# Two splits of the memory's weights, traced two steps later in the last pair's attention tail

## The chip, the cores and the metric

The kernel runs on one core of a Trainium2 chip. The metric is the device time of one execution in microseconds (us). TensorE is PE in the profile, its weight loads are PEld, VectorE is DVE, ScalarE is ACT, GpSimd is POOL, and SyncE, which issues the transfers here, is SP.

## The reference

One layer of a streaming encoder runs for two request groups with the same weights: a prompt of 1024 rows and a sample of 64 rows with caches. All inputs are float32. What matters for the change:

```
h = rms_norm(x, g_norm1)
qa, ka, va, qb, kb, vb, logf = in_proj(h, w_in, ...)       # 8 heads A, 8 heads B
oa = chunk_band_attn(qa, ka, va, rel_bias)                 # heads A
ob = forget_attn(qb, kb, vb, logf)                         # heads B: causal, logit += c[t] - c[s]
x = x + concat(oa, ob) @ w_o
kv = rms_norm(mem, g_mem) @ w_mkv                          # mem: 256 x 1024, w_mkv: 1024 x 2048
mk, mv = rms_norm(kv[:, :1024]), kv[:, 1024:]
x = x + mem_attend(rms_norm(x, g_norm2), mk, mv, w_mq, g_mq, w_mo)
x = x + conv_ffn(rms_norm(x, g_norm3), ..., w_up, w_conv, b_conv, w_down)
```

## The kernel before, in words

Every float32 product is made of three matmuls on two-part operands: an operand is split into a rounded high part and the rest, its low part (`hi` and `lo` in the names), and `SPLIT` lists the products hi·hi, hi·lo, lo·hi. A split takes a cast on ACT (the high part) and a subtraction on DVE or POOL (the low part).

The heads are worked in eight pairs. For a pair and a group of 256 query rows, attention has these steps, each a small function:

- `Attn.score` (lines 474 to 509): for heads B, POOL adds the forget term to a bias row (L485, `s<-bias,ctok`) and masks the diagonal block (L486). PE makes the scores (L499, `S<-kh,q`) in a PSUM tile `S` of which there is one. DVE adds bias and scores and takes the maximum (L502, `s,mx<-S,s`), ACT takes the exponential (L504), DVE the reciprocal of the sum (L505), and POOL (L507) or ACT (L509) divides by it.
- `Attn.turn` (L539 to L541): PE transposes the probabilities (`PT<-ident,s`), ACT and DVE split them into `pth` and `ptl`.
- `Attn.sum` (L554 to L566): PE multiplies them with the values into the PSUM tile `O`, of which there is one; ACT copies one half out (L563, `otmp<-O`), DVE adds the halves (L564, `mix<-O,otmp`), and a transfer stores `mix` to DRAM. The next head's L554 can write `O` only when L564 has read it.

The last pair's attention is left over when the projections are done. It is worked in four leftover steps, `LEFT = (0, 0, 0, 15)`: `step(n, substeps())` interleaves the steps of attention with `n` pieces of the next stage. In front of these steps the memory stage is opened: `load_mem` loads the memory's rows (a tile `s`) and splits them into `mhi` and `mlo` (L265, L266: `gained`), and `load_wm(n, z)` loads half a block of `w_mkv` into `mwraw` (two buffers, 512 KB each, L661). `split_wm(n, y)` splits a quarter of block `n`:

```
    def split_wm(n, y):
        raw = wraw[n, y // 2][:, 2 * (y % 2):2 * (y % 2) + 2]
        hi = mp.tile([P, 2, 256], F32R, name="mwhi", bufs=6)
        lo = mp.tile([P, 2, 256], F32R, name="mwlo", bufs=6)
        act.copy(hi, raw)
        (dve if y % 2 else pool).tensor_tensor(lo, raw, f32(hi), op=ALU.subtract)
```

The cast is L668 and the subtraction L669. The products of the memory stage (L679, `pj<-mwhi,mhi` and the like) are 16 units of 24 matmuls, cut into 64 pieces, of which 15 belong to the last leftover step and the rest to the sample attention that follows (`Sample`, L720 to L851: keys `kraw`, L740, split at L774 and L775). A unit's end (L695 to L713) makes a normed row `kv`, and PE transposes it at L710 during the next unit.

The order of the text is not the order on the engines. A scheduler in the framework places the traced instructions: it takes them by their place in the trace and by when it expects their inputs, and fixes a row of instructions for each engine and for SP. On the chip each engine runs its row in order and waits at a semaphore where an input is late. So a call that is traced elsewhere can move its neighbours too.

Of the kernel before, what the change touches and what calls it, by code (L numbers as in the profile page):

```python
# [26 lines left out]
LEFT = (0, 0, 0, 15)  # L27
# [14 lines left out]
def hybrid_step(ctx: ExitStack, tc: tile.TileContext, i: dict, o: dict):  # L42
# [3 lines left out]
    def f32(ap):  # L46
        return ap.bitcast(F32)
# [522 lines left out]
    def substeps(slow=False):  # L570

        sc = todo[0].scores() if todo else []
        va = late.pop(0).values() if late else []
        if todo:
            late.append(todo.pop(0))
        ns, ts = [x for x, _ in turns], [x for _, x in turns]
        turns.clear()
        first = held[:]
        held[:] = ts if slow else []
        r = first[:1] + ns + first[1:] + sc[:1] + ends if slow else first + sc[:1] + ends + ns  # L580
        r += va[:1] + sc[1:] + va[1:-1] + ([] if slow else ts)
        ends[:] = va[-1:]
        return [f for f in r if f]
# [69 lines left out]
    def load_mem(z):  # L653
        raw = wk.tile([P, N], F32, name="s", bufs=4)[:, :1024].rearrange("p (k t) -> p k t", k=4)
        nc.sync.dma_start(raw, i["memT"][4 * z:4 * z + 4].rearrange("k p t -> p k t"))
        for k in range(4):
            gained((mem[0][:, 4 * z + k], mem[1][:, 4 * z + k], raw[:, k], gcol[:, 3, 4 * z + k:4 * z + k + 1], ALL))
# [6 lines left out]
# [6 lines that stand above are left out]
        wm.setdefault(n, []).append((hi, lo))  # L670
# [201 lines left out]
    def step(n, subs):  # L872
        weave(line[:n], subs)
        del line[:n]
# [2 lines left out]
    load_mem(0)  # L877
    load_wm(0, 1)
    load_mem(1)
    split_wm(0, 0)  # L880
    split_wm(0, 1)
    for n in LEFT:
        step(n, substeps())
    assert not (todo or late or turns or ends)
    heads.close()
# [409 lines left out]
    def long_row(tag):  # L1295
        return row(tag, 768)[:, :H]
# [27 lines left out]
    for w, m in enumerate(ROWS):  # L1324
        x = long_row("qhi")
        nc.sync.dma_start(x, x1d[m, :, 0:H])
        for q in range(2):
            n = 2 * w + q
# [148 lines left out]
    for n, m in enumerate(ROWS):  # L1477
        x = long_row("qhi")
# [415 lines left out]
```

## Time and profile before

| | |
|---|---|
| time, median of 3 runs | 1781.4 us (1781.03 to 1784.44) |
| profiled execution | 1788.58 us, of which the span is 1786.6 us |
| mean granted TensorE clock | 0.988 |
| PE busy | 1717.5 us (96%) |
| DVE, ACT, POOL busy | 1210.5, 941.2, 647.3 us |
| last pair's attention tail, about 571 to 599 us | PE busy 0.38 of the first 8 us, 4.73 of the next 6, 10.82 of the last 14 |

The profiled execution is 7.2 us longer than the median of the runs; differences are worked out against the profiled execution and then taken off the median. In the timelines below the columns are: start in us, duration in us, engine, line, operation, output<-input, and in brackets the idle time of the engine before it and what ended it. With `x3` the row merges three instructions in a row, and the duration is that of all.

### The profile page before, as it was taken

The numbers are of one execution on the slowest core, as the hardware profiler recorded it, in microseconds if no ns is written. First come the engines' busy times: TensorE is split into PE (matmuls) and PEld (weight loads), VectorE is DVE, ScalarE is ACT, GpSimd is POOL, SyncE is SP. The second block draws the span as 40 slices with busy tenths as digits, with TensorE's granted clock in tenths as the row PEclk, the third lists the DMA queues.
The fourth block names the chain that finished last, engine by engine and source line by source line (L and its number), as shares of the span: only waits on it lengthen the run. The fifth ranks groups of instructions, "written<-read, shape, count | busy, mean of one in ns | idle before, by whom it ended". The sixth has DMA issues, their size and how long they took to land.

```text
span 1786.6 us, 33930 instructions
## 1 busy us (share of the span) xinstructions
PE 1717.5 (96%) x12432; PEld 1668.3 (93%) x12432; DVE 1210.5 (68%) x2643; ACT 941.2 (53%) x2058; POOL 647.3 (36%) x931
## 2 busy tenths in 40 slices
PE   7898999999998898999999999999999999999999
PEld 6888999999997777999999999999999999999999
DVE  5768667677677686433444369877777777649986
ACT  6756667677677577433555456434333333434432
POOL 4556667778777443453443612100000000000000
PEclk8999999999999999999999999999999999999999
DMA  7322222122112777541111563222222222693332
GB/s 251 91 62 64 60 77 78 49 74 76 51 56 83 216 252 219 165 143 56 54 54 60 151 214 104 79 75 77 79 85 85 85 73 73 216 346 130 118 104 88
DMA packets 134391, 199.87 MB, mean 112 GB/s; under 512 B 20984, under 2 KB 74360, under 8 KB 134224
## 3 DMA queue, kind: packets, MB, share of 16 engines
q1 hardware_dynamic: 134224, 197.70, 35.0%
q8 instruction: 98, 1.61, 0.4%
q14 instruction: 69, 0.57, 0.1%
HBM read 155.35 MB, written 45.44 MB: 112 GB/s over the span
## 4 chain that ended last, share of the span: by engine, by line
PE 46%; DVE 4%; issue 2%; ACT 1%; POOL 1%; DMA 1%; SPq 0%; DVEq 0%; ACTq 0%; POOLq 0%
PE W L1449 24%; PE W L1773 11%; PE pj L937 7%; PE S L1192 1%; PE tq L1228 1%; PE O L1228 1%; POOL lo L920 1%; DVE f L1314 0%; PE PT L1215 0%; DMA f<-x2d 0%; DVE lo L920 0%; DMA h<-ad 0%; PE O L1192 0%; ACT hi L1313 0%; DVE qhi L1301 0%
## 5 line engine op out<-in xcount | busy, mean ns | idle before, releaser
L299 PE MATMUL pj<-whi,xhi 128*128 128x384 f32 (+1 forms) x512 | 195.8, 382 | 2.7 <-DVE flog L314 1.6
L299 PE MATMUL pj<-wlo,xhi 128*128 128x384 f32 (+1 forms) x512 | 177.0, 346 | 4.3 <-POOL wlo L123 4.3
L299 PE MATMUL pj<-whi,xlo 128*128 128x384 f32 (+1 forms) x512 | 175.9, 344 | 0.7 <-DVE xlo L131 0.7
L1555 POOL COPY s<-gp 128x2 f32<-128x2 f32 x22 | 15.8, 720 | 335.8 <-DVE gp L1554 335.8
L1449 PE MATMUL W<-h,hi 128*128 128x272 f32 x704 | 134.4, 288 | 1.4 <-ACT qlo L1585 1.4
L504 ACT ACTIVATE s<-s,mx 128x640 f32<-128x640 f32 (+7 forms) x128 | 94.4, 737 | 77.4 <-DVE mx L502 76.5
L1773 PE MATMUL W<-f,hi 128*128 128x272 f32 x672 | 127.1, 287 | 0.1
L541 DVE TENSOR_TENSOR ptl<-PT,pth 128x512 fp32r<-128x512 f32 (+2 forms) x192 | 99.4, 522 | 37.5 <-ACT pth L540 35.3
L1449 PEld LDWEIGHTS W<-h,hi 128*128 128x128 f32 x704 | 110.8, 188 | 1.6 <-ACT qlo L1585 1.6
L540 ACT CAST pth<-PT 128x512 fp32r<-128x512 f32 (+2 forms) x192 | 84.7, 449 | 41.7 <-PE PT L539 39.9
L1773 PEld LDWEIGHTS W<-f,hi 128*128 128x128 f32 x672 | 105.3, 188 | 0.4 <-DVE f L1520 0.4
L299 PEld LDWEIGHTS pj<-wlo,xhi 128*128 128x128 f32 x512 | 99.5, 194 | 5.9 <-POOL wlo L123 5.9
L299 PEld LDWEIGHTS pj<-whi,xhi 128*128 128x128 f32 x512 | 99.4, 194 | 4.3 <-DVE flog L314 1.9
L1449 PE MATMUL W<-h,lo 128*128 128x272 f32 x352 | 101.8, 289 | 0.0
L299 PEld LDWEIGHTS pj<-whi,xlo 128*128 128x128 f32 x512 | 98.3, 192 | 1.4 <-DVE xlo L131 1.2
L1773 PE MATMUL W<-f,lo 128*128 128x272 f32 x336 | 96.7, 288 | 0.0
L539 PE MATMUL PT<-ident,s 128*128 128x128 f32 x528 | 89.9, 277 | 6.9 <-DVE ptl L541 5.4
L1313 ACT CAST hi<-raw 128x512 fp32r<-128x512 f32 x68 | 42.2, 621 | 98.6 <-PE W L1449 59.2
L499 PE MATMUL S<-kh,q 128*128 128x256 f32 (+1 forms) x304 | 77.8, 281 | 13.5 <-DVE mx L502 13.5
L937 PE MATMUL pj<-a,hi 128*128 128x384 f32 (+1 forms) x352 | 89.3, 337 | 0.2 <-DMA mraw<-mixd 0.2
L507 POOL TENSOR_SCALAR s<-s,ssum 128x640 f32<-128x640 f32 (+6 forms) x96 | 70.8, 738 | 47.9 <-DVE ssum L505 34.3
L554 PE MATMUL O<-pth,v 128*128 128x256 f32 (+1 forms) x304 | 76.5, 277 | 8.5 <-DVE mix L564 7.7
(538 smaller groups left out, 6037.6 us busy)
## 6 DMA issues: line engine op xcount, KB each, us to landing
raw<-in_w_down_dram SPq DMA_DIRECT2D x45, 256.0 KB, 2.8
wraw<-in_w_dram SPq DMA_DIRECT2D x56, 192.0 KB, 2.5
raw<-in_w_up_dram SPq DMA_DIRECT2D x41, 256.0 KB, 2.8
h<-ad SPq DMA_DIRECT2D x32, 272.0 KB, 5.5
mwraw<-in_w_mkv_dram SPq DMA_DIRECT2D x16, 512.0 KB, 6.1
raw<-in_w_mo_dram SPq DMA_DIRECT2D x32, 256.0 KB, 3.2
kvraw<-in_w_down_dram SPq DMA_DIRECT2D x32, 256.0 KB, 3.0
ad<-t SPq DMA_DIRECT2D x22, 272.0 KB, 2.2
```

The source lines that it names most:

```text
L299: pe.matmul(pj[:, :nw], x2[a][:, k, t * P:(t + 1) * P], wt[k][b][:, :nw], start=n == 0, stop=n == 3 * KT - 1)
L499: pe.matmul(sp[:, a:a + (k1 - k0) * P], q, kk[:, h, src], start=m == 0, stop=m == 1)
L504: act.activation(s[:, :n], s[:, :n], ACT.Exp, bias=mx, scale=-1.0, accum_out=sm)
L507: pool.tensor_scalar(s[:, :n], s[:, :n], sm, 1.0, op0=ALU.mult, op1=ALU.mult)
L539: pe.transpose(pt[:, b - ch[0]], self.s[j][:, (b - w0) * P:(b - w0 + 1) * P], ident)
L540: act.copy(hi[:, f:f + n, j], pt[:, f:f + n])
L541: dve.tensor_tensor(lo[:, f:f + n, j], pt[:, f:f + n], f32(hi[:, f:f + n, j]), op=ALU.subtract)
L554: pe.matmul(op[:, cols], groups[p, b // 2].v[:, b % 2, h].rearrange("p a d -> p (a d)"), pt[:, x, cols], start=b == self.full[0] and m == ...
L937: pe.matmul(out()[:, :cn], w[a][:, k % 4], x[b][k][:, c0:c0 + cn], start=k == 0 and n == 0, stop=k == KT - 1 and n == 2)
L1313: act.copy(hi, t)
L1449: pe.matmul(w[:, z, :Q], a(p, j), rights[j][b][:, z * Q:z * Q + Q], start=fresh and begin and j == 0 and x == 0, stop=final and end and j ...
L1773: pe.matmul(ws[m][:, z, :Q], la[p][:, m * P:(m + 1) * P], ra[b][:, z * Q:z * Q + Q], start=first and y == 0 and what in opening, stop=fina ...
```

## The change

The first two of the memory's splits, `split_wm(0, 0)` and `split_wm(0, 1)`, are traced in front of the third leftover step instead of in front of the first. The rest of the opening (the loads, and the splits of the memory's rows) stays where it was.

```diff
     load_mem(0)
     load_wm(0, 1)
     load_mem(1)
-    split_wm(0, 0)
-    split_wm(0, 1)
-    for n in LEFT:
+    for x, n in enumerate(LEFT):
+        if x == 2:
+            split_wm(0, 0)
+            split_wm(0, 1)
         step(n, substeps())
```

No instruction is added or taken away. The rows of all engines differ only from this place on, until early in the product with `w_o` about 150 us later. From line 880 on the changed kernel's line numbers are higher by one; line numbers here are those of before.

ACT, from the splits of the first half of the memory's rows (`mhi`) on, before:

```order
L265 ACTIVATE mhi<-s,gcol 128x256 x3
L668 CAST mwhi<-mwraw 128x512 x2
L563 COPY otmp<-O 64x256
L540 CAST pth<-PT 128x4x128 x2
L668 CAST mwhi<-mwraw 128x512 x2
L265 ACTIVATE mhi<-s,gcol 128x256 x4
L504 ACTIVATE s,ssum<-s,mx 128x896
```

ACT at the same place after:

```order
L265 ACTIVATE mhi<-s,gcol 128x256 x3
L563 COPY otmp<-O 64x256
L540 CAST pth<-PT 128x4x128 x2
L668 CAST mwhi<-mwraw 128x512 x2
L540 CAST pth<-PT 128x128
L668 CAST mwhi<-mwraw 128x512
L540 CAST pth<-PT 128x2x128
L265 ACTIVATE mhi<-s,gcol 128x256 x4
L504 ACTIVATE s,ssum<-s,mx 128x896
```

The first two casts of the weights have moved from in front of `otmp` to behind it and two casts of probabilities. Later on ACT (not shown) the casts of the next block's first two quarters stand between the last head's casts of `pth`, where before they stood ahead of the third exponential.

DVE from the same place on, before (L502 is the pass that adds bias and scores, its second row reads out the maximum):

```order
L266 SCALAR_TENSOR_TENSOR mlo<-s,gcol,mhi 128x256 x3
L669 TENSOR_TENSOR mwlo<-mwraw,mwhi 128x512
L564 TENSOR_TENSOR mix<-O,otmp 64x256
L502 ISA s,mx<-S,s 128x896
L502 ISA mx 128x1
L541 TENSOR_TENSOR ptl<-PT,pth 128x4x128
L266 SCALAR_TENSOR_TENSOR mlo<-s,gcol,mhi 128x256 x4
L541 TENSOR_TENSOR ptl<-PT,pth 128x4x128
L505 RECIPROCAL ssum<-ssum 128x1
L502 ISA s,mx<-S,s 128x1024
```

DVE after, from the same place in two pieces; the first is the opening:

```order
L266 SCALAR_TENSOR_TENSOR mlo<-s,gcol,mhi 128x256 x3
L564 TENSOR_TENSOR mix<-O,otmp 64x256
L541 TENSOR_TENSOR ptl<-PT,pth 128x4x128 x2
L502 ISA s,mx<-S,s 128x896
```

The second follows a few rows later:

```order
L266 SCALAR_TENSOR_TENSOR mlo<-s,gcol,mhi 128x256 x4
L502 ISA s,mx<-S,s 128x1024
L502 ISA mx 128x1
L505 RECIPROCAL ssum<-ssum 128x1
L564 TENSOR_TENSOR mix<-O,otmp 64x256
L669 TENSOR_TENSOR mwlo<-mwraw,mwhi 128x512 x2
L505 RECIPROCAL ssum<-ssum 128x1
L502 ISA s,mx<-S,s 128x896
```

The subtraction of the weights has left its place in front of the first `mix`; it stands now together with a second one behind the second `mix`, in front of the second reciprocal and the third L502.

POOL, from the last small product of the projections (`ko`) on, before:

```order
L256 TENSOR_TENSOR ko<-qk,gk 64x128
L485 TENSOR_SCALAR s<-bias,ctok 128x896
L669 TENSOR_TENSOR mwlo<-mwraw,mwhi 128x512
L486 AFFINE_SELECT s<-s 128x128
L669 TENSOR_TENSOR mwlo<-mwraw,mwhi 128x512
L485 TENSOR_SCALAR s<-bias,ctok 128x1024
L486 AFFINE_SELECT s<-s 128x128
L485 TENSOR_SCALAR s<-bias,ctok 128x896
```

POOL at the same place after:

```order
L256 TENSOR_TENSOR ko<-qk,gk 64x128
L485 TENSOR_SCALAR s<-bias,ctok 128x896
L486 AFFINE_SELECT s<-s 128x128
L669 TENSOR_TENSOR mwlo<-mwraw,mwhi 128x512
L485 TENSOR_SCALAR s<-bias,ctok 128x1024
L485 TENSOR_SCALAR s<-bias,ctok 128x896
L486 AFFINE_SELECT s<-s 128x128 x2
L485 TENSOR_SCALAR s<-bias,ctok 128x1024
```

The first mask has come in front of the weights' subtraction, and the second mask has gone behind the third bias row.

SP's queue around the first sample's keys, before (L699 stores a unit's normed row, L713 its transpose, L727 and L729 load the sample's query and value):

```order
L713 DMA kmd<-kt 128x2x128
L729 DMA svn<-sv 64x128
L740 DMA kraw<-in_cbk_dram 128x1024
L699 DMA out_mk_dram<-kv 128x256
L713 DMA kmd<-kt 128x2x128
L740 DMA kraw<-in_cbk_dram 128x1024
```

SP's queue at the same place after, from the same transfer on:

```order
L713 DMA kmd<-kt 128x2x128
L727 DMA sqd<-sqk 64x512
L729 DMA svn<-sv 64x128
L699 DMA out_mk_dram<-kv 128x256
L740 DMA kraw<-in_cbk_dram 128x1024
L713 DMA kmd<-kt 128x2x128
L740 DMA kraw<-in_cbk_dram 128x1024
```

The first sample's first keys (`kraw`) now stand behind the store of the third unit's row. Further up in the queue (not shown) the load of the next block's first weights (`mwraw`) moves from in front of three loads of attention results (`mraw`) to behind them and behind the store of the second `mix`.

## The prediction

> **What bounds the kernel now.** I read the page first, then the stretches around the change, then the timeline of each engine there.
>
> ```profile
> span 1786.6 us, 33930 instructions
> PE 1717.5 (96%) x12432; PEld 1668.3 (93%) x12432; DVE 1210.5 (68%) x2643; ACT 941.2 (53%) x2058; POOL 647.3 (36%) x931
> ```
>
> PE is busy for 96% of the span and no matmul is added or removed, so the change can only win or lose PE's idle time, 69 us in all (1786.6 - 1717.5). The stretches show how much of it lies where the order differs.
>
> ```profile
> core 0: us, PE busy (x) PEld busy (x) DVE busy (x) ACT busy (x) POOL busy (x), PEclk, DMA share, GB/s
> 571.00:579.00 8.00, 0.38 (x4) 0.14 (x2) 5.73 (x9) 6.71 (x16) 6.37 (x10) 0.68 0.67 224
> 579.00:585.00 6.00, 4.73 (x19) 3.88 (x19) 4.89 (x10) 3.27 (x7) 3.35 (x5) 0.57 0.89 318
> 585.00:599.00 14.00, 10.82 (x77) 9.02 (x78) 10.51 (x23) 10.49 (x19) 7.54 (x10) 1.00 0.72 206
> 599.00:620.00 21.00, 17.86 (x142) 16.83 (x141) 14.28 (x36) 8.53 (x27) 10.30 (x15) 1.00 0.56 165
> 620.00:640.00 20.00, 16.32 (x106) 13.45 (x105) 15.07 (x37) 14.41 (x35) 8.50 (x8) 1.00 0.83 277
> ```
>
> From 571 to 599 PE is idle for 12.1 us (28 - 0.38 - 4.73 - 10.82), and in part of it its clock is halved (0.57). This is the last pair's attention, a chain from engine to engine. One wait carries most of it; here are PE, ACT, DVE and POOL at that place:
>
> ```profile
> 570.32 1.06 PE L539 MATMUL PT<-ident,s 128*128 128x128 f32 x8
> 579.07 0.55 PE L554 MATMUL O<-pth,v 128*128 128x256 f32 x1 [7.69 <-DVE mix L564]
> ...
> 574.31 1.14 ACT L668 CAST mwhi<-mwraw 128x512 fp32r<-128x512 f32 x2 [1.24 <-DMA mwraw<-in_w_mkv_dram]
> 575.47 0.37 ACT L563 COPY otmp<-O 64x256 f32<-64x256 f32 x1
> ...
> 572.30 1.28 DVE L266 SCALAR_TENSOR_TENSOR mlo<-s,gcol,mhi 128x256 fp32r<-128x256 f32 x3
> ...
> 575.48 3.00 DVE L669 TENSOR_TENSOR mwlo<-mwraw,mwhi 128x512 fp32r<-128x512 f32 x1 [1.89 <-ACT mwhi L668]
> 578.51 0.42 DVE L564 TENSOR_TENSOR mix<-O,otmp 64x256 f32<-64x256 f32 x1
> ...
> 575.25 0.45 POOL L256 TENSOR_TENSOR ko<-qk,gk 64x128 f32<-64x128 f32 x1
> 575.69 1.01 POOL L485 TENSOR_SCALAR s<-bias,ctok 128x896 f32<-128x896 f32 x1
> 576.66 1.26 POOL L669 TENSOR_TENSOR mwlo<-mwraw,mwhi 128x512 fp32r<-128x512 f32 x1
> 577.89 0.74 POOL L486 TENSOR_SCALAR_AFFINE_SELECT s<-s 128x128 f32<-128x128 f32 x1
> ```
>
> PE ends its transposes at 571.38 and waits 7.69 us for `mix`. `mix` stands on DVE behind the weights' subtraction (3.00 us), that one behind two casts on ACT, and these behind a transfer that lands at 574.3. `otmp` waits behind the same casts.
>
> **The change, link by link.** The moved work is two casts on ACT and one subtraction each on DVE and POOL; its loads stay. The sum asks when each later link comes, against before.
>
> Link 1, the wait itself. With the casts behind it, `otmp` follows the third `mhi` at about 573.1 (ACT was idle for 1.24 us up to 574.31), `mix` follows the last `mlo` at 573.6 and ends at 574.0, and PE goes on at 574.1: idle for 2.7 us instead of 7.7. That is 5 us at this link. It is not 5 us at the end, because the next link has another releaser.
>
> Link 2, the first long softmax pass (L502). It needs POOL's mask, and POOL starts its bias row at 575.69 in both kernels, after `ko`, which the moved casts do not feed. New: bias row to 576.70, mask in front of the subtraction, 0.29 us by the row below: 577.0.
>
> ```profile
> 578.85 1.07 DVE L502 CUSTOM_DVE_ANT_0 s<-S,s 128x896 f32<-128x896 f32 x1
> ...
> 580.46 1.66 DVE L266 SCALAR_TENSOR_TENSOR mlo<-s,gcol,mhi 128x256 fp32r<-128x256 f32 x4
> ...
> 583.89 1.22 DVE L502 CUSTOM_DVE_ANT_0 s<-S,s 128x1024 f32<-128x1024 f32 x1 [1.11 <-POOL s L486]
> ...
> 585.58 1.29 DVE L669 TENSOR_TENSOR mwlo<-mwraw,mwhi 128x512 fp32r<-128x512 f32 x1
> ...
> 586.87 1.06 DVE L502 CUSTOM_DVE_ANT_0 s<-S,s 128x896 f32<-128x896 f32 x1
> ...
> 582.37 1.12 POOL L485 TENSOR_SCALAR s<-bias,ctok 128x1024 f32<-128x1024 f32 x1 [2.50 <-PE PT L539]
> 583.57 0.29 POOL L486 TENSOR_SCALAR_AFFINE_SELECT s<-s 128x128 f32<-128x128 f32 x1
> 583.84 1.02 POOL L485 TENSOR_SCALAR s<-bias,ctok 128x896 f32<-128x896 f32 x1
> ...
> 587.04 1.12 POOL L507 TENSOR_SCALAR s<-s,ssum 128x1024 f32<-128x1024 f32 x1
> ...
> 588.13 1.73 POOL L669 TENSOR_TENSOR mwlo<-mwraw,mwhi 128x512 fp32r<-128x512 f32 x1
> ```
>
> L502 came at 578.85 and comes at 577.0 now: 1.8 us are left of the 5.
>
> Link 3, the second L502 (583.89 before). POOL's row in front of its mask is now: subtraction 1.26, bias row 1.12, the third bias row 1.02, then the mask 0.29, so 577.0 + 3.7 = 580.7, and the gain would be 3.2 us. But DVE's four `mlo` (1.66 us with POOL idle) now run from 578.7 to 580.4 beside these POOL rows, and the two disturb each other: the subtraction of 575.48 took 3.00 us beside three POOL rows, the mask of 577.89 took 0.74 instead of 0.29, and the POOL subtraction of 588.13 took 1.73 instead of 1.26. If a subtraction waits for the end of the POOL row under way and the next POOL row then waits for it, the four `mlo` (0.41 each) alternate with bias row, mask and mask: 579.4 (end of the second bias row) + 4 x 0.41 + 1.02 + 2 x 0.29 = 582.6. The gain at this link is 3.2 us undisturbed, 1.2 us disturbed. The Trainium skill, SBUF — State Buffer, section Who interferes with whom, says that a DVE instruction with two SBUF inputs contends with a GpSimd instruction that reads SBUF, and that the loser waits for the whole instruction; the 3.00 us agrees. By it the disturbed value holds here, without it the other.
>
> Link 4, the third L502 (586.87 before). Two subtractions of weights now stand in front of it, where before only one did, and one of POOL's falls beside them. Disturbed: the second L502 ends at 583.9, reciprocal and `mix` at 584.4, the first subtraction waits for POOL's until 585.4, both end at 586.5, the reciprocal at 586.7. Gain 0.2 us. Undisturbed, with the shortest such subtraction for each (row below):
>
> ```profile
> 615.11 0.68 DVE L669 TENSOR_TENSOR mwlo<-mwraw,mwhi 128x512 fp32r<-128x512 f32 x1
> ...
> 590.93 0.16 DVE L505 RECIPROCAL ssum<-ssum 128x1 f32<-128x1 f32 x1
> ```
>
> 580.7 + 1.2 + 0.6 (reciprocal and `mix`) + 2 x 0.68 + 0.16 = 584.0, a gain of 2.8 us.
>
> Link 5, the rest of the tail, is led by L502, exponential, division, transposes and ends where the memory's products start:
>
> ```profile
> 596.00 0.97 ACT L540 CAST pth<-PT 128x512 fp32r<-128x512 f32 x2
> ...
> 595.94 0.42 DVE L564 TENSOR_TENSOR mix<-O,otmp 64x256 f32<-64x256 f32 x1 [0.66 <-ACT otmp L563]
> ...
> 598.69 0.28 PE L679 MATMUL pj<-mwhi,mhi 128*128 128x256 f32 x1
> ```
>
> The two casts that left ACT ahead of the third exponential (1.1 us, like the pair at 574.31) come back between the last casts of `pth`, and one subtraction comes in front of the last head's `mix`: up to 0.5 us at each place. Their load is issued behind DVE's first subtraction now, at about 586, and lands 3.7 us later by the median of the row below, before ACT asks for it at about 592: hidden behind the softmax, and if that cover is gone, up to the 1.24 us of the stall at 574.31.
>
> ```profile
> mwraw<-in_w_mkv_dram SPq DMA_DIRECT2D x5, 512.0 KB, 3.7
> ...
> 587.01 0.33 SPq L661 DMA_DIRECT2D mwraw<-in_w_mkv_dram  x1
> ```
>
> So the memory's products start at about 598.2 disturbed (gain 0.5 us, and -0.5 if the last `mix` loses another POOL row) and at 596.3 undisturbed (gain 2.4). I take 1.0, nearer to the disturbed end, since the two long rows above are of just this kind.
>
> The halved clock. PE's last matmul ended at 571.38 and the stretch shows 0.68 up to 579, so 8 x (1 - 0.68) x 2 = 5.1 us of it ran at half, and it halved at about 573.9, 2.5 us after. An idle time of 2.7 us ends at that edge. I count nothing: until 585 PE is not the link that comes last, since POOL's masks come later than the scores in the working above. The Trainium skill, TensorE: Matmul & The Clock Gate, Part 1, gives an idle window of about 3.4 us, by which 2.7 us would not halve the clock; the trace's 2.5 us is shorter, and the sum is the same by both.
>
> The stage behind it, 599 to 720. The same matmuls stand in another mixture with the samples' attention. What can be won or lost are waits like these:
>
> ```profile
> PE PT L710 <- DVE kv L698: 3.5, 4, 1.3
> ...
> 612.82 0.58 SPq L740 DMA_DIRECT2D kraw<-in_cbk_dram  x1
> ...
> 615.22 0.34 SPq L699 DMA_DIRECT2D out_mk_dram<-kv  x1
> ...
> 621.46 1.14 ACT L774 CAST kchi<-kraw 128x512 fp32r<-128x512 f32 x2 [2.97 <-DMA kraw<-in_cbk_dram]
> ```
>
> For the better: at the third unit ACT's two steps of the norm are no longer parted by a cast, and half of the 3.5 us of waits for `kv` could go, 1.8 us. For the worse: the first sample's keys are issued behind the store of 615.22, 2.4 us later, and their first matmul stands only nine memory matmuls (1.1 us) later. The second keys keep their place, and ACT waited 2.97 us for these. I count 0 for this stage, with +1.8 and -2.4 as its ends.
>
> **Sum.** 1788.58 - 1.0 = 1787.6 us for the profiled execution; off the median, 1781.4 - 1.0 = 1780.4 us.
>
> **Rivals.** 0.2% of the median is 3.6 us, about what a measurement of this kernel can tell from no change.
>
> Faster: subtractions and POOL rows do not collide, 2.4 us of the tail's 5 survive, and the waits for `kv` shrink by 1.8: 4.2 us, 1777.2. For it: 5 us are truly taken off the largest single wait of the tail, and undisturbed subtractions of 0.68 us occur (615.11). Against: the POOL row of 575.69, which nothing moves, caps the first gain at 1.8.
>
> Slower: the first sample's keys decide. If they land 2.4 us later, PE meets them too early; and with the transfer engines busy for 0.83 of 620 to 640 the loads of the next sample, which follow in the same queue, cannot catch up, so that the second sample is as late as the first: 2 x 2.4, less the 1.0 of the tail, is 3.8 us, 1785.2. It decides from the point where PE has worked off the nine memory matmuls that now stand ahead and waits for `kchi` by more than 1.3 us (2.4 less 1.1). Against: the second keys are not issued later, and they are the ones that ACT waited for.
>
> That the scheduler puts the splits back where they were is excluded by the rows of ACT and DVE above.
>
> **How the numbers follow.** Within 0.2%: 0.58, since the worked range of the tail is -0.5 to +2.4. Faster by more: 0.27, which needs the good end of both stages. Slower by more: 0.15. The range runs from 1776.5 (the good ends, 4.2 us, and a little of the runs' own spread) to 1785 (the bad ends, 2.9 us, and the spread of 3 us that the three runs show upwards, in part). The likeliest case's own range is 1778 to 1784.
>
> **What the changed profile would show.** Link 1 right: PE's wait for the first `mix` shrinks from 7.7 to about 2.7 us. Link 2: L502 of 896 columns at 577.0. Link 3: its successor near 582.6, with `mlo` x4 well over 1.66 us; at 580.7 if I am wrong on the collision. Link 4: two weights' subtractions in a row on DVE, the first over 1 us. The end of the tail: the first L679 between 596.3 and 599.2. The forecast is wrong if the clock stays low into the memory's products, or if PE waits for `kchi` at the first sample by over 3 us in all.

## The result, and the profile after

The changed kernel takes 1790.72 us (median of six runs, 1787.51 to 1791.63) against 1782.04 us before (1780.52 to 1786.0): a ratio of 1.0041 over all the runs, 95% interval 1.0029 to 1.0053, about 7.3 us slower (the two medians alone are 8.7 us apart). The forecast was 1780.4 with 1776.5 to 1785.0 as its range; the time lies above the range, on the side that had been given 0.15. Timed again at the end of the study, the ratio was 1.0045 (1.0033 to 1.0058).

The profiled execution after takes 1790.69 us. The page's head:

```profile
span 1788.7 us, 33936 instructions
PE 1720.7 (96%) x12432; PEld 1671.5 (93%) x12432; DVE 1214.5 (68%) x2643; ACT 940.6 (53%) x2058; POOL 643.5 (36%) x931
```

Set beside the first profile of before this shows 2 us and explains nothing: that execution (1788.58 us) was 7 us above its kernel's median. I therefore profiled before again (1784.47 us, span 1782.5). In the second profile every engine has the same rows in the same order, as it must; from 120 us to 566 us the first runs 2.7 us behind it, lost ahead of 120 us, where both kernels are the same, and between 575 and 830 us its rows keep that distance to within 0.8 us. All differences below are against the second profile. They are the start of the same matmul in both traces, set to zero at 548 to 566 us, where the kernels don't differ yet; + is later. The columns are places in the program, by the time that the second profile of before has there; the first column has the kernels:

| | tail's end 590-599 | first norm 603-611 | 626-640 | 660-690 | 715-735 | `w_o` 740-800 | 815-850 |
|---|---|---|---|---|---|---|---|
| after | -0.2 | +0.9 | +1.6 | +2.0 | +1.2 | +5.1 | +6.3 |
| after, profiled again | -0.2 | +0.9 | +2.3 | +2.8 | +1.9 | +3.9 | +4.1 |

Behind 850 us the difference stays, 6.2 us at 1700 us, in the first trace; the second adds 1.2 more. So the tail that the change was aimed at wins 0.2 us, the samples' attention behind it loses 1.4 to 2.0, and the product with `w_o`, 150 us behind the edit, loses 2.0 to 3.9. The base is one execution, though. The same rows in two other traces of before stand at +0.4 us (the first profile) and -1.5 us (a version below that differs only behind 730 us) at 715 to 735, so what this table gives for the samples' stage is uncertain by about 1.5 us. The step at `w_o` is firmer: the first profile moves by 0.1 us there.

The tail went link by link much as worked out. The timeline of after is shown; its `ko`, the row that nothing moves, starts 2.78 us earlier (572.47, against 575.25 in the prediction's rows), so 2.78 is added to compare:

```profile
571.84 0.58 PE L554 MATMUL O<-pth,v 128*128 128x256 f32 x1 [3.23 <-ACT pth L540]
...
574.31 1.09 DVE L502 CUSTOM_DVE_ANT_0 s<-S,s 128x896 f32<-128x896 f32 x1 [1.69 <-POOL s L486]
575.86 3.03 DVE L266 SCALAR_TENSOR_TENSOR mlo<-s,gcol,mhi 128x256 fp32r<-128x256 f32 x4
578.81 1.21 DVE L502 CUSTOM_DVE_ANT_0 s<-S,s 128x1024 f32<-128x1024 f32 x1
580.59 2.28 DVE L669 TENSOR_TENSOR mwlo<-mwraw,mwhi 128x512 fp32r<-128x512 f32 x2
582.86 1.06 DVE L502 CUSTOM_DVE_ANT_0 s<-S,s 128x896 f32<-128x896 f32 x1
586.52 1.22 DVE L502 CUSTOM_DVE_ANT_0 s<-S,s 128x1024 f32<-128x1024 f32 x1 [1.77 <-PE S L499]
...
595.74 0.28 PE L679 MATMUL pj<-mwhi,mhi 128*128 128x256 f32 x1
...
572.47 0.45 POOL L256 TENSOR_TENSOR ko<-qk,gk 64x128 f32<-64x128 f32 x1
```

PE's wait of 7.69 us is down to 3.23, and what ends it is the cast of `pth` on ACT, no longer `mix`. `mlo` x4 is at 3.03 us instead of 1.66 (the collision with POOL's rows), and the passes L502 start at 577.1, 581.6 and 585.6 on before's scale. A new wait follows: the fourth L502 waits 1.77 us for PE's scores. The stretches show why:

```profile
core 0: us, PE busy (x) PEld busy (x) DVE busy (x) ACT busy (x) POOL busy (x), PEclk, DMA share, GB/s
571.00:579.00 8.00, 5.80 (x23) 4.95 (x23) 6.24 (x12) 6.30 (x15) 7.47 (x13) 0.50 0.70 223
579.00:585.00 6.00, 3.87 (x16) 3.29 (x17) 5.57 (x10) 3.94 (x7) 3.76 (x4) 0.50 0.70 245
585.00:599.00 14.00, 12.27 (x84) 10.78 (x84) 7.21 (x14) 7.53 (x16) 5.12 (x6) 0.90 0.67 197
599.00:620.00 21.00, 18.39 (x132) 17.29 (x132) 14.13 (x36) 9.62 (x31) 9.30 (x15) 0.92 0.64 193
620.00:640.00 20.00, 16.69 (x105) 14.53 (x104) 17.72 (x41) 15.09 (x36) 9.07 (x8) 0.91 0.86 275
...
740.00:760.00 20.00, 19.41 (x106) 19.44 (x107) 7.71 (x11) 7.11 (x15) 10.25 (x9) 0.91 0.46 145
```

PE works sooner, but at half clock: 0.50 in all of 571 to 585. Of before's two stretches 5.1 and 6 x 0.43 x 2 = 5.2 us ran at half, 10.3 us in all; here it is 14 + 14 x 0.10 x 2 = 16.8 us. And from 585 on, where before has 1.00 in each of these stretches, all four shown stand at 0.90 to 0.92. The first of them is the end of the tail's own half clock, which lasts until 587.9; the other three hold a new fall each. A share of 0.91 in 20 us is 20 x 0.09 x 2 = 3.6 us at half clock, one window of the clock (last section). At `w_o` the second profile of before has full clock all through:

```profile
740.00:760.00 20.00, 20.00 (x123) 20.00 (x122) 6.80 (x12) 7.72 (x15) 9.29 (x9) 1.00 0.52 164
```

The largest single loss is early in the product with `w_o`. SP's queue and what hangs on it, before (the prediction's profile) and after:

```profile
735.46 0.33 SPq L911 DMA_DIRECT2D raw<-in_w_o_dram  x1
735.89 0.37 SPq L1066 DMA_DIRECT2D qhi<-in_xT_dram  x1
736.71 0.33 SPq L911 DMA_DIRECT2D raw<-in_w_o_dram  x1
...
739.48 0.56 DVE L1073 TENSOR_TENSOR qhi<-pj,qhi 128x384 f32<-128x384 f32 x1 [0.80 <-DMA qhi<-in_xT_dram]
```

```profile
733.72 2.54 SPq L912 DMA_DIRECT2D raw<-in_w_o_dram  x2
736.37 0.37 SPq L1067 DMA_DIRECT2D qhi<-in_xT_dram  x1
...
734.62 1.29 POOL L921 TENSOR_TENSOR lo<-raw,hi 128x512 fp32r<-128x512 f32 x1
...
739.88 0.56 DVE L1074 TENSOR_TENSOR qhi<-pj,qhi 128x384 f32<-128x384 f32 x1 [2.93 <-DMA qhi<-in_xT_dram]
...
740.59 0.59 PE L938 MATMUL pj<-a,hi 128*128 128x384 f32 x2 [2.08 <-DVE qhi L1074]
```

`raw` has its weights loaded into a buffer that POOL's subtraction (`lo`) must have read; `qhi` is the residual that is added to the product, and its load had nothing of its own to wait for. Before, it goes out between two loads of `raw`. After, both loads of `raw` stand ahead, the second waits in the queue until POOL's `lo` of 734.62 is done, and the residual waits behind it without need. DVE's addition then waits 2.93 us for the transfer, and PE 2.08 us for DVE; before, PE did not wait here. None of this code was edited: the scheduler's order slipped.

### The profile page after: what moved, and what is told of

It reads as the page before. It is cut to its first block, busy times and chain, and to the rows that moved or that the text cites. A ratio compares the mean times of both kernels' runs of the same rounds, so it can differ in the third digit from the quotient of the medians.

```text
span 1788.7 us, 33936 instructions
## 1 busy us (share of the span) xinstructions
PE 1720.7 (96%) x12432; PEld 1671.5 (93%) x12432; DVE 1214.5 (68%) x2643; ACT 940.6 (53%) x2058; POOL 643.5 (36%) x931
## 5 line engine op out<-in xcount | busy, mean ns | idle before, releaser
L540 ACT CAST pth<-PT 128x512 fp32r<-128x512 f32 (+2 forms) x192 | 84.6, 449 | 42.9 <-PE PT L539 41.3
L539 PEld LDWEIGHTS PT<-ident,s 128*128 128x128 f32 x528 | 66.2, 142 | 17.1 <-DVE ptl L541 9.7
```

Source lines behind the costliest of these rows:

```text
L539: pe.transpose(pt[:, b - ch[0]], self.s[j][:, (b - w0) * P:(b - w0 + 1) * P], ident)
L540: act.copy(hi[:, f:f + n, j], pt[:, f:f + n])
```

## The experiments

The experiments change rows only. A pin is a dependency between two instructions of one engine (or of SP's queue) that the scheduler must keep and that costs no wait on the chip; the two names are output tiles, the first row goes first. In the expectations Q is the loss at SP's queue, N that at the first norm of the samples' stage, K that through the order of the sample's loads. The number that opens each result is the ratio of the version's time to that of before, with its 95% interval. Places and differences in us are those of the table above, from one trace of each version. The lists of pins are printed in short form, and a pin names its tiles by the numbers that they have in the version at hand.

```diff
+def pin(tc):
+    for first, then in PINS:
+        first, then = find(tc, *first), find(tc, *then)
+        tc.add_manual_dep(then, first.name, mybir.DependencyInfo(
+            mybir.DependencyClass.NoSync, mybir.DependencyReason.DATA), reason="order")
```

**Before, profiled again.** No edit.

> The kernel before, unchanged, profiled once more, to learn whether the first profiled execution (1788.58 us, against a median of 1782.0) shows the usual course. If the 2.4 us that it lost ahead of 120 us, with the clock halved from about 61 to 68 and 95 to 98 us, were chance, this one ends near 1782 to 1784 us and the stretch 575 to 830 us is the same row for row; if the first profile is typical, it ends near 1788 us again and the timed runs differ from profiled ones by some 6 us.

1784.47 us; it gave the base of the table above.

**The residual's load first again, in after.**

```diff
+PAIR = ('qhi_10818', 'raw_10811')
```

`PAIR` is one such pin, of two loads on SP; the versions with several use `PINS`.

> The kernel after, in which only one row of SP's queue stands where it stood before: the load of the residual of the output product's second group is issued ahead of the second weight load that waits for its buffer. Theory Q (the loss is the queue: the residual's load stood behind a weight load that waits for POOL's subtraction, so that PE waited 2.08 us for its accumulator and then ran at half clock for about 3 us): 3.0 to 3.9 us faster than after, 1787 us or 3 to 5 us over before, and no PE wait over 0.5 us at that place. Theory T (the loss is made by the moved splits themselves in the softmax tail and the samples' stage, with the longer halved clock): within 1 us of after, 1790 us, since PE only loses there what it has saved elsewhere.

1.0025 (1.0016 to 1.0035), from 1.0041 and 1.0045. PE's wait went from 2.08 to 0.66, and the difference at 740 to 800 from +5.1 (+3.9) to +1.6 us:

```profile
737.04 0.59 PE L938 MATMUL pj<-a,hi 128*128 128x384 f32 x2 [0.66 <-DVE qhi L1074]
```

**The residual's load last, in before.**

```diff
+PAIR = ('raw_10811', 'qhi_10818')
```

> The kernel before with nothing moved but SP's queue at the output product: the residual's load of the second group is put behind the second weight load, as the changed kernel has it. Theory Q: PE waits about 2 us for the accumulator there, the clock may halve for 3.4 us, and the kernel is 2.0 to 3.9 us slower than before (1784 to 1786 us). Theory T: no difference over 1 us from before, because the product there has slack.

1.0014 (1.0005 to 1.0022): the slip alone makes the old kernel slower. SP's row and PE's:

```profile
730.28 1.58 SPq L911 DMA_DIRECT2D raw<-in_w_o_dram  x2
...
732.44 3.30 SPq L1066 DMA_DIRECT2D qhi<-in_xT_dram  x2
...
736.54 0.58 PE L937 MATMUL pj<-a,hi 128*128 128x384 f32 x2 [1.58 <-DVE qhi L1073]
```

The difference goes from -1.5 us at 715 to 735 to +0.9 at 740 to 800: 2.3 us. (The -1.5 is chance: no row differs ahead of the pin. It arises between 611 and 646 us, where both traces have full clock, in waits of PE that came out shorter.)

**The splits moved by one step instead of two.**

```diff
-        if x == 2:
+        if x == 1:
```

> Both splits one leftover step later than before instead of two: the tail of the softmax is changed less, and SP's queue at the output product has the same order as in after. Theory Q: most of the loss is there all the same, 3 to 7 us slower than before (1785 to 1789 us), with the same PE wait of about 2 us at the output product. Theory T: the loss shrinks with the move, to under 2 us over before (1784 us or less).

1.0029 (1.002 to 1.0038). Another tail, the same order of SP at `w_o`, and PE waits 1.77 us there; +1.7 at 715 to 735, +3.7 behind it. So neither loss needs the two steps: the scheduler falls into the same order at `w_o` from another edit.

**The first norm: POOL's mask ahead of the weights' subtraction, in after.** The samples' stage makes its first normed row in a chain of DVE steps of 128x1. In the timeline of after two of them take 1.1 us, beside two rows of POOL, and PE waits 2.02 us for the row:

```profile
604.48 0.41 PE L710 MATMUL PT<-ident,kv 128*128 128x128 f32 x2 [2.02 <-DVE kv L698]
...
625.23 1.41 PE L822 MATMUL PT<-ident,s 128*128 128x128 f32 x6 [1.85 <-ACT s L808]
...
617.12 1.14 ACT L774 CAST kchi<-kraw 128x512 fp32r<-128x512 f32 x2 [1.47 <-DMA kraw<-in_cbk_dram]
...
601.54 1.14 DVE L79 SCALAR_TENSOR_TENSOR rsq_a<-rsq_a,rsq_y 128x1 f32<-128x1 f32 x1
602.71 1.10 DVE L80 SCALAR_TENSOR_TENSOR mr<-rsq_a,rsq_y 128x1 f32<-128x1 f32 x1
...
601.34 1.32 POOL L669 TENSOR_TENSOR mwlo<-mwraw,mwhi 128x512 fp32r<-128x512 f32 x1 [1.45 <-issue]
602.64 1.16 POOL L762 TENSOR_SCALAR s<-s,stok 128x1088 f32<-128x1088 f32 x1
```

The same rows in before (second profile), where only the step ahead of these two, L78, is held by POOL (1.26 us):

```profile
603.96 0.41 PE L710 MATMUL PT<-ident,kv 128*128 128x128 f32 x2 [1.27 <-DVE kv L698]
...
624.38 0.87 PE L822 MATMUL PT<-ident,s 128*128 128x128 f32 x6 [0.93 <-ACT s L808]
...
615.23 1.12 ACT L774 CAST kchi<-kraw 128x512 fp32r<-128x512 f32 x2
```

L762 of after adds the sample's mask, which in before stands ahead of that subtraction.

```diff
 PINS = [(('SP', 'qhi_10818'), ('SP', 'raw_10811')),
+        (('Pool', 's_9288'), ('Pool', 'mwlo_8962'))]
```

> The kernel after with the residual's load ahead as in the run before it, and one more row put back: on POOL the mask addition (L762) of the third sample tile stands ahead of the first weight subtraction of the memory's second quarter unit, as before, not between the two subtractions. Theory N (two POOL rows in a row, 601.34 to 603.80, hold two of DVE's 128x1 steps of the norm at 1.14 and 1.10 us, PE waits 2.02 us instead of 1.27 for the first normed keys, and this idle time is what halves the clock for 3.4 us behind it): about 0.7 us of wait and 1.3 to 1.6 us of halved matmuls come back, 1.5 to 2.3 us faster than the version with the residual's load alone (ratio to before near 1.001). Theory S (slack: PE catches up in the samples' attention, where DMA and ACT set the pace): no more than 0.5 us faster.

1.0020 (1.0011 to 1.0029), not to be told from the version before it. The wait did not shrink, it grew to 2.46 us: with the mask gone, two subtractions of POOL stood side by side, and the same two DVE steps again lay beside them.

```profile
601.41 2.49 POOL L669 TENSOR_TENSOR mwlo<-mwraw,mwhi 128x512 fp32r<-128x512 f32 x2
...
604.59 0.41 PE L710 MATMUL PT<-ident,kv 128*128 128x128 f32 x2 [2.46 <-DVE kv L698]
```

**The first keys' load ahead of a store, too.**

```diff
+        (('SP', 'kraw_9105'), ('SP', 'out_mk_dram', 'kv_9037'))
```

> As the version with two rows put back, and on SP the load of the first sample's first keys stands ahead of the store of the third memory unit again. Theory K (my slower rival in another place: the keys' load 2.9 us later sends the casts of the keys, and by them the scores and the exponential, 0.9 us later, PE waits 1.85 us instead of 0.93 at L822 and the clock halves a second time): 1.0 to 2.0 us faster than with two rows, the halved stretch at about 625 us is gone, and the kernel is within 0.1% of before. Against it: once the norm ahead is quicker, the store no longer holds the queue, and this row is worth under 0.3 us.

1.0018 (1.0009 to 1.0027), no change that can be told. PE's wait for the sample's probabilities (L822) stayed, by the table of waits (sum, count, longest):

```profile
PE PT L822 <- ACT s L808: 1.7, 1, 1.7
```

**POOL's mask late, in before.** The norm's loss by itself.

```diff
+PINS = [(('Pool', 'mwlo_8962'), ('Pool', 's_9288'))]
```

> The kernel before with one row moved: on POOL the mask addition of the third sample tile behind the first weight subtraction of the second quarter unit. Theory N: DVE's norm steps meet two POOL rows, PE's first wait for the normed keys grows from 1.27 to about 2 us, and the clock halves behind it where the idle time fills more than half of one of its 3.4 us windows; 0.7 to 2.3 us slower than before. Theory S: within 0.5 us of before.

1.0014 (1.0005 to 1.0022). Now before has it too, in three steps:

```profile
602.33 1.26 DVE L78 TENSOR_TENSOR rsq_a<-mms,rsq_y 128x1 f32<-128x1 f32 x1 [0.88 <-ACT rsq_y L77]
603.63 1.10 DVE L79 SCALAR_TENSOR_TENSOR rsq_a<-rsq_a,rsq_y 128x1 f32<-128x1 f32 x1
604.76 1.20 DVE L80 SCALAR_TENSOR_TENSOR mr<-rsq_a,rsq_y 128x1 f32<-128x1 f32 x1
...
606.63 0.66 PE L710 MATMUL PT<-ident,kv 128*128 128x128 f32 x2 [3.19 <-DVE kv L698]
```

In the trace the difference is +2.1 us at the norm and +1.0 from 715 on: half is given back in this stage (by which wait I did not work out). The ratio stands for 2.5 us, more than the trace shows.

**The second subtraction moved behind the mask's last row as well.**

```diff
 PINS = [(('SP', 'qhi_10818'), ('SP', 'raw_10811')),
         (('Pool', 's_9288'), ('Pool', 'mwlo_8962')),
+        (('Pool', 's_9288', '#last'), ('Pool', 'mwlo_9053'))]
```

> The version with two rows put back, and nothing else but one more row on POOL: the second weight subtraction of the second quarter unit stands behind the two memsets and the masks of the third sample tile (0.9 us of small rows), as before, instead of directly behind the first subtraction. The two-row version had put two subtractions side by side (601.41 to 603.90), so that DVE's 128x1 steps took 1.22 and 1.18 us again. Theory N (a 128x1 step of DVE ends only with the POOL row beside it): one step is long, one short, PE's wait for the first normed keys falls from 2.46 to 1.3 to 1.6 us, the window of halved clock behind it is gone, and the stretch from the tail to the output product is 1.5 to 2.5 us shorter than in the two-row version. Theory S (slack behind): the wait falls, but what is won is waited for again at L822 for the sample's exponential, and the stretch is less than 0.7 us shorter.

1.0019 (1.001 to 1.0027). One of the two steps takes 0.16 us again and the wait is 1.16:

```profile
601.10 1.22 DVE L79 SCALAR_TENSOR_TENSOR rsq_a<-rsq_a,rsq_y 128x1 f32<-128x1 f32 x1
602.35 0.16 DVE L80 SCALAR_TENSOR_TENSOR mr<-rsq_a,rsq_y 128x1 f32<-128x1 f32 x1
...
603.18 0.41 PE L710 MATMUL PT<-ident,kv 128*128 128x128 f32 x2 [1.16 <-DVE kv L698]
...
624.42 0.88 PE L822 MATMUL PT<-ident,s 128*128 128x128 f32 x6 [1.85 <-ACT s L808]
```

That won 1.45 us at 603 to 611 (-0.3 instead of +1.2), and at 626 to 640 the kernel stands at +0.8 again: PE waits 1.85 at L822, as in after. What the norm wins the next wait takes.

**PE kept busy in an idle time, in before.** A side question: 4.03 us of PE's idle time at 701 to 706 us, with the halved clock behind it, filled with twenty transposes whose result nobody reads.

```diff
+            for _ in range(20 if self.p == SAMPLES[-2] else 0):
+                pe.transpose(tq[:, 1], ident, ident)
```

> The kernel before with 20 transposes of the identity added in the idle time of PE at the end of the samples (701.3 to 705.6 us, waiting for the division of the sum), into a half of the bank that nothing reads. Theory H (a 3.4 us window in which PE is less than half busy halves the clock, and PE's own work behind it pays): the 10.2 us of halved clock at the start of the output product shrink to 3.4 us or none, PE's matmuls from 707 to 715 us run at full clock, and the kernel is 0.8 to 3.0 us faster than before. Against it, theory D (DVE's eight splits of the mixed heads, 1.23 us each, set the end there, 701.9 to 716.1 us): the clock stays up, and the time is the same within 0.5 us.

1.0010 (1.0001 to 1.0019), slower. The clock of 700 to 720 rose from 0.74 to 0.91 and about 1.2 us was won there (+0.7 at 690 to 707, -0.5 at 715 to 735), as meant:

```profile
700.00:720.00 20.00, 16.86 (x93) 14.90 (x92) 14.95 (x28) 14.00 (x30) 8.43 (x5) 0.91 0.66 223
```

But the order at `w_o` had slipped again, and 1.8 us was lost there (the line numbers of this version are two higher here):

```profile
730.56 2.87 SPq L913 DMA_DIRECT2D raw<-in_w_o_dram  x2
...
737.53 0.59 PE L939 MATMUL pj<-a,hi 128*128 128x384 f32 x2 [1.55 <-DVE qhi L1075]
```

**The same, with the residual's load pinned.**

```diff
+PINS = [(('SP', 'qhi_10838'), ('SP', 'raw_10831'))]
```

> The kernel before with the 20 transposes in PE's idle time at the end of the samples, and on SP the residual's load of the second group ahead of the second weight load that waits for its buffer. In the run with the transposes alone the stretch up to the output product was 1.1 us shorter and then 1.8 us were lost, with a PE wait of 1.55 us, at exactly that load, since the row had slipped behind. Theory Q: the wait falls below 0.7 us and the kernel is 0.8 to 1.8 us faster than before in the stretch (1782 to 1783.5 us where before has 1784). Theory F (a first-in-first-out queue of residual loads that paces the product anyway): the 1.1 us are lost at the next residual's load instead, and the time is that of before within 0.5 us.

0.9991 (0.9982 to 1.0000), 1783.07 us beside 1784.3: the best of all versions, at the edge of what these runs can tell. No wait at `w_o` is left.

**After with the samples' loads at before's places, too.**

```diff
 PINS = [(('SP', 'qhi_10818'), ('SP', 'raw_10811')),
         (('Pool', 's_9288'), ('Pool', 'mwlo_8962')),
         (('Pool', 's_9288', '#last'), ('Pool', 'mwlo_9053')),
+        (('SP', 'sqd_9098'), ('SP', 'out_mk_dram', 'kv_8987')),
+        (('SP', 'kraw_9105'), ('SP', 'out_mk_dram', 'kv_9037'))]
```

> The version with mask and split put back, and SP's queue at the first sample as it was before: the load of its queries ahead of the store of the second memory unit, its first keys ahead of the store of the third. By the profiles the first keys are cast 1.7 us later than before (against the first memory product), the exponential 0.7 us later, and PE waits 1.85 us at L822 instead of 0.93. Theory K (the sample's chain sets the pace of this stage, and its loads stand behind stores that wait for the norm): the first cast of the keys comes 1.0 to 2.0 us earlier, the wait at L822 falls to about 1 us, the halved clock at about 625 us goes, and against the kernel before the stretch from the tail to the output product comes out between -0.5 and +0.5 us (it was +1.2 in the version without this row, +1.2 to +2.0 in after). Theory M (it is the other mixture of memory products and sample work on PE and ACT that costs, not the loads): the loads come earlier, and the stretch stays at +0.8 or more.

1.0001 (0.9992 to 1.001): with queue, norm and loads put back, the whole loss is gone, as far as these runs can tell, though the splits stay where the change put them. The first keys' cast comes at before's place in the program (616.77 against 615.23, in a trace whose first L679 also starts 1.5 us later), yet the wait at L822 is still 1.79, and the trace keeps +1.0 us, hardly less than the version without these two rows (+1.2). The scheduler changed PE's row along with them, so this is not the loads alone:

```profile
616.77 1.14 ACT L774 CAST kchi<-kraw 128x512 fp32r<-128x512 f32 x2 [0.84 <-DMA kraw<-in_cbk_dram]
...
627.20 1.01 PE L822 MATMUL PT<-ident,s 128*128 128x128 f32 x6 [1.79 <-ACT s L808]
```

**All of it and the transposes, in after.** The five pins of the last kernel and the twenty transposes.

> The kernel after with all rows put back (mask, split, first sample's loads, residual's load) and the 20 transposes: what the move is worth in the tail alone, with the clock kept up at the end of the samples. By the sum of the stretches: -0.3 (tail), 0 (samples, by theory K; +1.0 by theory M), -1.1 (transposes): 1 to 1.5 us faster than before by K, the same as before by M.

0.9998 (0.9989 to 1.0006). It is not better than before with transposes and one pin: the change brings nothing that can be told even where all that it lost is put back. (The two traces are 1.8 us apart the other way, -1.3 against +0.6 behind 740. The other one had lost 1.8 us in its tail, see the last section.)

**The samples' loads late, in before.**

```diff
+PINS = [(('SP', 'out_mk_dram', 'kv_8987'), ('SP', 'sqd_9098')),
+        (('SP', 'out_mk_dram', 'kv_9037'), ('SP', 'kraw_9105'))]
```

> The kernel before, in which on SP the load of the first sample's queries stands behind the store of the second memory unit, and its first keys behind the store of the third, as in the changed kernel (its values' loads slip ahead of the keys with it, so the keys come later still). Theory K (the queue at the first sample costs): first cast of the keys 1.5 to 4 us later, a wait of PE of 1.8 us or more in the first sample, 1.5 to 4 us slower than before. Theory M (the mixture of matmuls, not these loads): within 0.7 us of before.

1.0008 (0.9999 to 1.0017); +1.1 us in the trace. The loads of the sample's values slipped as well, so the first keys' cast came at 621.02, more than the move of the keys' load alone was to give. PE's row changed too: the first sample's scores now stand behind 129 memory matmuls instead of 111. So this run does not part theory K from theory M.

**The samples' loads early, in after, and nothing else.**

```diff
+PINS = [(('SP', 'sqd_9098'), ('SP', 'out_mk_dram', 'kv_8987')),
+        (('SP', 'kraw_9105'), ('SP', 'out_mk_dram', 'kv_9037'))]
```

> The kernel after with only the two rows of SP at the first sample put back (queries ahead of the second store, first keys ahead of the third). The order of SP at the output product goes back to that of before by itself with it, though nothing there is touched. Theory K: these two rows carry nearly all of the loss, their own part of about 3 us and the 3 to 4 us of the output product's queue; the kernel is within 1.5 us of before, 6 us faster than after. Theory M: only the output product's part comes back, 3.5 us, and it stays 3 to 4.5 us slower than before, like the version with the residual's load alone (1.0025). Theory N (POOL's rows at the first norm, which stay as in after): 2 us of the loss stay.

1.0012 (1.0003 to 1.0022). It is not a test of the loads alone: PE's row changes as in the version with five pins, and with these two rows the scheduler's order at `w_o` came back to before's by itself (`qhi` between two loads of `raw`) and no wait is left there, while the norm's wait stays (2.0 us). The trace stands at +2.5 to +2.6 us from 660 to 800.

**After, timed and profiled again.** No edit.

> The kernel after, unchanged, profiled once more, to part what every execution shows from what one showed. Of its 6.3 us against the kernel before (between the last softmax scores and 860 us), 3.9 lie at the output product's residual load, 1.2 in the samples' stage and 1.2 at 816 us, behind a halved clock that none of the variants shows. If the last is chance (an idle time that one window of the clock takes in whole), it is gone and the stretch costs 5.1 us; the first two stand again, each within 0.7 us. If it belongs to the change, it is there again.

1.0045 (1.0033 to 1.0058). The same two losses stand again, the one at `w_o` with 2.0 us instead of 3.9, which is more than the 0.7 allowed for: the wait there was 1.7 us without a halved window behind it. The +1.1 of the first trace at 815 us is gone, so that one was chance.

```profile
PE pj L938 <- DVE qhi L1074: 1.7, 1, 1.7
```

## Why the prediction was wrong

- **Links 1 to 4 were right in the main.** PE's wait: 2.7 worked out, 3.23 measured, but with another releaser, the cast of `pth` on ACT (L540) instead of `mix`. L502: 577.0, and 577.1 measured. For the next two the working gave a value with the collision of DVE and POOL and one without, and the measured ones lie halfway: 582.6 or 580.7, and 581.6; 586.7 or 584.0, and 585.6. The collision itself is there: `mlo` x4 took 3.03 us beside POOL's rows and 1.66 with POOL idle. The rule that the Trainium skill gives (SBUF — State Buffer, section Who interferes with whom) agrees with this.
- **Link 5, the 1.0 us, was mis-sized.** First L679 at 595.74 + 2.78 = 598.5 against 598.69: the tail gained 0.2. Of the 1.2 us that the third L502 still had (586.87 - 585.64), 0.5 was left at the fourth (589.79 - 589.30), which waited 1.77 us for PE's scores.
- **"I count nothing" for the halved clock failed.** PE did become the releaser: the wait of 3.23 us and thin work kept the clock at half for 16.8 us instead of 10.3. The eight score matmuls ahead of the fourth L502 start 1.2 us earlier than before (584.34 + 2.78 against 588.30), but at half clock they take 2.05 us instead of 1.20, and only 0.3 is left at their end. The working had looked at whether the clock falls, not at when it comes back. Its sign "wrong if the clock stays low into the memory's products" did not come true as worded: full clock was back at 587.9, 8 us ahead of the first of these products, and fell again later, at 604.9 and 625.4, for one window each.
- **The stage behind, counted 0 with ends +1.8 and -2.4, was the first of the two large errors.** It measured a loss of 1.4 to 2.0, within the ends, but the term was set to nothing. The gain that was counted came: the waits for `kv` (L710) shrank from 3.5 us in four (4.1 in the second profile) to 2.2 in two. It was outweighed. From the first L679 to the first matmul with `w_o` PE is idle for 14.7 us in after and 13.2 in the second profile of before, and 9.5 us against 3.1 of that stage run at half clock. Two places were not in the working: the first norm, where POOL's mask and subtraction swap places and so hold DVE's steps of 128x1 (late mask rows alone cost before 1.0 us in the trace, ratio 1.0014), and the wait at L822 (two points down).
- **Nothing was counted behind 720 us: the second and largest error.** The order of the rows was known to differ up to the product with `w_o`, and no term was set for it, neither price nor bound. Its cost is 2.0 to 3.9 us in the traces, shown from both sides: taken out of after (1.0041 and 1.0045 to 1.0025), and put into before (1.0014).
- **The slower rival had the place and not the mechanism.** The first sample's keys did come later (cast at 617.12 against 615.23, in two traces that agree at 548 to 566), and PE's wait at L822 grew from 0.93 to 1.85. But putting the loads back left the wait at 1.79. The traces point at PE's own row: between the sample's last scores from its keys (L797) and L822 stand 16 memory matmuls in before, 8 in after, and 5 with the loads put back. In the six traces with 16 the wait is 0.74 to 0.93 us, in the six with 8 it is 1.84 to 1.86, in the one with 9 it is 1.75, in the three with 5 it is 1.78 to 1.92. Eight matmuls, started 0.12 us apart, are 0.95 us, which is what the wait grew by: PE has worked them off ahead of the scores and has nothing left while ACT makes the exponential. No run put PE's row back by itself, so this is read from the traces and not tested. The rival's condition (a wait for `kchi` of over 1.3 us) was not met in after, with 0.6 us; in the repeat it was 1.3 us in three waits.

What stays open: how much of the loss in the samples' stage each of these places carries, since PE's row was never put back alone; and why the runs' ratios of some variants differ by 1 to 3 us from what the stretches of their one profiled execution show. After itself has 7.3 us by the runs, 6.3 and 4.1 in the traces. With the residual pinned, 1.0025 is 4.5 us and the trace shows 1.8 (this execution, 1784.27 us, was the shortest of its eleven). The two rows of the sample's loads are worth 3 us by the runs (1.0019 to 1.0001) and 0.2 in the traces. A profile is one draw of the clock's windows and of the waits.

## What to carry to other kernels

Where a scheduler fixes the order, an edit's price lies wherever the order differs, not where the code does: list every place that differs, up to the last, and set a term or a bound for each, SP's queue above all. In a queue that issues in order, a load whose buffer is still being read holds back every load behind it: put the loads that wait for nothing ahead of it. And shortening an idle time did not bring a halved clock back here; only dense work did.

## What the runs showed of the hardware

**The clock goes by windows, and half a window idle is enough.** In the clock records of all 17 traces, stretches at half clock are whole multiples of 3.41 us (but for the last one, in which the kernel ends). Cut into windows of that length, with PE's busy time from the matmul records: at full clock a window in which PE was busy for under 0.45 was followed by half clock in 72 of 73 cases, at 0.45 to 0.5 in 14 of 21, at 0.5 to 0.55 in 7 of 40, at 0.55 to 0.6 in 1 of 31, above 0.6 in 2 of some 8500. At half clock, full clock came back after none of 81 windows busy under 0.8, after 2 of 18 at 0.8 to 0.85, after 13 of 18 at 0.85 to 0.9, and after all 76 above 0.9. The Trainium skill (TensorE: Matmul & The Clock Gate, Part 1) tells of a free-running window of about 3.4 us and of a fall after an idle one; the length agrees, but a fully idle window is not needed: in after, 2.08 us of idle time up to 740.59 were followed by a halved window from 741.46 on. In the repeat 1.7 us at the same place were not. Since the windows' phase differs between executions, the same rows at `w_o` cost 2.0 us in one and 3.9 in another. That this is most of a kernel's spread is my guess, which no run here shows.

**A pair on DVE and POOL can come out either way.** In the second profile of before the two subtractions of weights at about 585 us took 0.84 us on DVE and 1.73 on POOL; in the version with transposes, whose rows there are the same, 1.72 and 1.29, and the tail ended 1.7 us later. All five traces of before without the transposes show the first outcome (0.75 to 0.84 on DVE) and both with them the second (1.72), so whether it is chance or belongs to the transposes is not shown.

**A small DVE step can last as long as the POOL row beside it.** A step of 128x1 takes 0.16 us alone and, at the first norm, up to 1.26 us beside a POOL row: the chain of three in before with the late mask took 3.56 us (1.26, 1.10 and 1.20). Such a step ended with the POOL row: in the version with three pins the step of 601.10 ends at 602.32, and POOL's subtraction that started at 601.01 and took 1.29 us ends at 602.30.
